# Twenty-one chunks of u turned by VectorE beside the mixer, not eighteen, at starts listed one by one

## The chip, the core and the metric

One core of a Trainium2 chip runs the kernel. The metric is the device time of one execution in microseconds (us). Three runs of the kernel before took 941.5, 942.26 and 942.73 us; their median is 942.26 us. The engines are named as in the profile: PE is TensorE, PEld its weight loads, DVE is VectorE, ACT is ScalarE, POOL is GpSimd, SP is SyncE, which here only issues transfers. ACT issues transfers too; "ACTq" and "SPq" mark these in the timelines.

## What is computed

One decoder layer on 256 tokens of width 1024, all in float32:

```python
h = rmsnorm(x, mix_norm_g[l])
proj = h @ w_in[l]
rq, rk, rv, rg, mq, mk, mv, ga, gb = jnp.split(proj, offsets, axis=-1)
...
y_a = (from_heads(ret) * jax.nn.silu(rg)) @ ret_w_branch[l]
...
y_b = from_heads(att) @ moba_w_branch[l]
merged = jax.nn.sigmoid(ga) * y_a + jax.nn.sigmoid(gb) * y_b
x = x + merged @ w_out[l]
h2 = rmsnorm(x, ffn_norm_g[l])
x = x + peer(h2, peer_w_q[l], peer_sub_keys[l], peer_u[l], peer_v[l])
```

`ret` is retention over two chunks of 128 tokens, `att` block-sparse attention. `peer` picks 16 of 16384 experts for each token and head, by keys:

```python
u = u_tab[ec]
a = jax.nn.gelu(jnp.einsum('td,thkd->thk', hc, u), approximate=False)
return jnp.einsum('thk,thkd->td', gc * a, v_tab[ec])
```

## The kernel before

The program is one stream of instructions for each engine, in the order of the code; what an engine has issued is never overtaken on that engine. The work has four stages.

**The mixer** (0 to about 240 us): everything up to `x + merged @ w_out`. Its weights are cut into 72 pieces, each 256 rows by 512 columns, held as 128 partitions x 1024. The first pieces are those of the attention's q, k and v, then come the retention's q, k and v (12 to 27), the merge gates and the swish gate (28 to 51), the branch weights (52 to 63) and w_out (64 to 71). Pieces 64 to 67 make the left half of the output columns, 68 to 71 the right half.

**The queries** (to about 300 us): 16 more pieces, w_q, handled in the same way.

**The u stage** (303.5 to about 650 us): all products of the tokens with the 128 chunks of u, 128 rows each. PE needs each chunk with its rows along the free axis. So for a plain chunk it first makes eight 128 x 128 transposes (L738, `transpose_u`), which ACT copies out of PSUM in two steps (L739), and then the products (L1290).

**The v stage** (about 650 to 930 us): the products with the 128 chunks of v (L1322 and L1323), and a tail.

Around the u and v stages POOL and DVE gather and treat rows for some of the tokens; the change touches none of that.

*The loop of the mixer* (L844) takes the pieces i in order, and its body sets the order of all queues:

```python
for i in range(n_mixer + 3):
    load_to(i + 1)
    ...
    cut(i + 3)
    products(i)
    early_turns(i)
    pump()
```

- `load_to` has SP load weights (L203) into a ring of six raw tiles, and goes four pieces ahead of the one that it is called for.
- `cut(i + 3)` splits a piece into an upper part, which ACT copies (`rhi`, L148), and a lower part, which DVE subtracts (`rlo`, L149); there are four of each, numbered on in the names that the trace prints. A piece's three products a tile (upper by upper, and both cross products) are L231 to L233 or L240 to L242.
- `products(i)` issues PE's work on piece i and, at the last piece of a unit, starts the unit's epilogue, a generator that goes on a step at each `pump()`. Two such generators matter here. `retention` makes scores, multiplies them by the decay on DVE in two halves (`st`, L431), multiplies by v on PE (L442) and normalises; ACT scales the result (`ret`, L462). `residual` adds the last products to the residual stream (`xt`, L563), weights it by the gain (`xg`, L567), both on DVE, and PE transposes it (L576) for the queries.
- `early_turns(i)` prepares chunks of u for the u stage. For such a chunk ACT issues four loads (L748, the quarters of the chunk, one for each 32 partitions and 128 KB each), DVE transposes the chunk in blocks of 32 x 32, in two half-turns at two successive i (`STREAM_TRANSPOSE`, L752, 128 x 512 each), and ACT issues the store of the turned chunk (L764) to a tensor in device memory. There are two pairs of buffers, `eraw` to `eT` and `h` to `hTf`, used by turns. A chunk's loads go out when the chunk before it starts its first half-turn. The loads of the next use of a buffer wait for the half-turns of the last one, and the half-turns into `eT` or `hTf` wait for its last store.

In the kernel before, chunk number m (0 to 17) makes its first half-turn at i = 14 + 3m, its second one piece later, its store two pieces later, and its loads go out three pieces earlier. Turned are the chunks 6, 13, 20 and so on to 125: one in seven (`STEP`). The u stage loads these from where they were stored (`turned[c // STEP]`) and leaves out L738 and L739 for them.

Of the kernel before, what the change touches and what calls it, by code (L numbers as in the profile page):

```python
# [50 lines left out]
HELD = [0, 1, 2, 8, 14, 21] + list(range(26, 62, 6)) + [61, 66]  # L51
HELD0 = 2
FOLD = 48
NPRE = 18
STEP = 7
PRE0 = 14
PERIOD = 3
TURN = ()
WARM = 8
GROW = 96  # L60
# [16 lines left out]
def layer_kernel(ctx, tc, x, mix_norm_g, w_in, ret_w_branch, moba_q_gain, moba_k_gain, moba_w_branch,  # L77
                 rel_bias, w_out, ffn_norm_g, peer_w_q, peer_sub_keys, peer_u, peer_v,
                 c_rope, c_decay, c_col, c_bucket, out, dbg=None):
    nc = tc.nc  # L80
# [23 lines left out]
    def raw_tile(n=1):  # L104

        i = raw_count[0] % RAWS
        raw_count[0] += n
        assert i + n <= RAWS
        return raw_ring[:, i] if n == 1 else raw_ring[:, i:i + n]
# [62 lines left out]

    turned = dr.tile([NPRE, P, D], F32, name="turned")
    ident = cp.tile([P, P], F32, name="ident")
# [37 lines left out]
    def products(i):  # L212
# [30 lines left out]
        if k0 + 2 == kc:  # L243
# [11 lines left out]
    early = ([ap.tile([P, D], F32, name="eraw"), h2],  # L255
             [ap.tile([P, D], F32, name="eT"), hTf.rearrange("p k t -> p (k t)")[:, :D]])
# [433 lines left out]
    def load_any(i):  # L690
# [9 lines left out]
        elif i < len(pieces) + NK:  # L700
# [3 lines left out]
            if early_chunk(c):  # L704
                u_raw[c] = raw_tile()
                nc.sync.dma_start(u_raw[c], turned[c // STEP])
            elif c in TURN:
# [33 lines left out]
    def early_chunk(c):  # L741
        return c % STEP == STEP - 1 and c // STEP < NPRE

    def load_quarters(queue, dst, c):

        src = peer_u[0, c * P:(c + 1) * P, :].rearrange("(b a) (g d) -> g a b d", a=32, g=4)
        for g in range(4):
            queue.dma_start(dst[32 * g:32 * g + 32].rearrange("a (b d) -> a b d", b=4), src[g])  # L748

    def turn(dst, src, k):  # L750

        V.transpose(dst.rearrange("p (k b a) -> p b k a", k=KC, b=4)[:, :, k],  # L752
                    src.rearrange("p (b k i) -> p b k i", b=4, k=KC)[:, :, k])

    def early_turns(i):

        m, step = divmod(i - PRE0, PERIOD)
        if step == 0 and -1 <= m < NPRE - 1:
            load_quarters(nc.scalar, early[0][(m + 1) % 2], STEP * (m + 1) + STEP - 1)
        if 0 <= m < NPRE:  # L760
            if step < 2:
                turn(early[1][m % 2], early[0][m % 2], slice(4 * step, 4 * step + 4))
            if step == PERIOD - 1:
                nc.scalar.dma_start(turned[m], early[1][m % 2])  # L764

    G.iota(jp, pattern=[[1, P]], base=0, channel_multiplier=-1)
# [559 lines left out]
    for c in range(NK):  # L1326
# [14 lines left out]
        if c == FOLD:  # L1341
            assert gs["sum"] >= NV - NJ
            for b in range(KC):
                s = slice(b % 4 * 32, b % 4 * 32 + 32)
# [111 lines left out]
```

## Time and profile before

| what | value |
|---|---|
| median of the three runs | 942.26 us |
| the profiled execution, its own time | 945.16 us |
| its span | 943.3 us |
| granted clock of PE | 1.0 |
| instructions | 19128 |
| moved | 322.56 MB, 342 GB/s over the span |
| transfers issued by ACT's queue (q10) | 21.29 MB, 7.5% of the 16 engines' span |

The page's slices give each engine's busy share in tenths over 40 equal stretches of the span, here 23.6 us each, and what the transfers moved:

```profile
PE   9999999999999999999999999999999999999997
...
DVE  6658557788678998999998999974978988899978
ACT  6544655544644435444687778776454636464443
...
DMA  9899779998799998999999999999999999999994
```

The mixer is the first ten digits. A timeline's row reads: start, duration, engine, line and operation, output and inputs; a count behind "x" is the number of records drawn together into one row. In square brackets stands how long the engine was idle before, and what came last of what it waited for.

### The profile page before, as it was taken

Reading aid. Unit: us, or ns where it says so; the run is one execution under the profiler, and the core shown is the slowest. Engines: PE = TensorE matmul, PEld = TensorE weight load, DVE = VectorE, ACT = ScalarE, POOL = GpSimd, SP = SyncE. Lnnn points to the kernel's source line nnn. Section 1 sums busy time; section 2 is a strip of 40 time slices with the busy share of each in tenths; the row PEclk is TensorE's granted clock in tenths of the full one; section 3 lists DMA queues with packets and bytes.
Section 4 is the critical chain, followed back from the end, with each engine's and each line's share of the span. In section 5 each row is a group of like instructions: output and inputs, shape, how many; then the busy total and the mean of one; then the engine's idle time right before and its main releaser. Section 6 shows DMA issues by size and latency. Waiting matters only on the chain.

```text
span 943.3 us, 19128 instructions
## 1 busy us (share of the span) xinstructions
PE 933.2 (99%) x7192; PEld 893.3 (95%) x7192; DVE 793.5 (84%) x1521; ACT 520.9 (55%) x953; POOL 399.6 (42%) x313
## 2 busy tenths in 40 slices
PE   9999999999999999999999999999999999999997
PEld 6887898998999999999999999999999999999996
DVE  6658557788678998999998999974978988899978
ACT  6544655544644435444687778776454636464443
POOL 3412010000202446534646677763546555575721
PEclk9999999999999999999999999999999999999999
DMA  9899779998799998999999999999999999999994
GB/s 320 232 235 283 241 206 291 303 300 264 244 363 379 403 402 274 403 406 359 377 398 391 377 363 382 377 386 364 362 357 402 409 377 367 406 402 392 409 337 134
DMA packets 111050, 322.56 MB, mean 342 GB/s; under 512 B 11660, under 2 KB 23861, under 8 KB 110830
## 3 DMA queue, kind: packets, MB, share of 16 engines
q1 hardware_dynamic: 64460, 184.38, 55.0%
q0 software_dynamic: 32752, 115.67, 32.5%
q10 hardware_dynamic: 13746, 21.29, 7.5%
q8 instruction: 57, 0.93, 0.4%
q14 instruction: 35, 0.29, 0.1%
HBM read 308.63 MB, written 14.19 MB: 342 GB/s over the span
## 4 chain that ended last, share of the span: by engine, by line
PE 85%; DMA 7%; DVE 3%; issue 2%; POOL 1%; ACT 1%; SPq 0%; DVEq 0%; ACTq 0%; POOLq 0%
PE acc L1290 24%; PE side L738 11%; PE acc L1322 7%; PE side L1322 7%; DMA raw_ring<-in_peer_v_dram 5%; PE acc L231 5%; PE acc L232 5%; PE acc L233 5%; PE acc L1323 3%; PE side L1323 3%; PE acc L240 3%; PE acc L241 3%; PE acc L242 3%; DMA bias<-skew 1%; PE acc L1218 1%
## 5 line engine op out<-in xcount | busy, mean ns | idle before, releaser
L1038 POOL DMA_INDIRECT rows<-in_peer_u_dram,eg x86 | 109.0, 1267 | 69.8 <-DVE rows L1049 32.6
L1038 POOL DMA_INDIRECT rows<-in_peer_v_dram,eg x54 | 99.8, 1849 | 74.2 <-DVE vacc L1124 47.9
L738 PE MATMUL side<-ident,raw_ring 128*128 128x128 f32 x768 | 103.0, 277 | 0.0
L738 PEld LDWEIGHTS side<-ident,raw_ring 128*128 128x128 f32 x768 | 93.0, 192 | 0.0
L1167 ACT ACTIVATE oh_buf<-oh_more,tS 128x128 bf16<-128x128 f16 x176 | 58.5, 417 | 0.5 <-issue 0.5
L1049 DVE SCALAR_TENSOR_TENSOR rows<-rows,h 128x1024 f32<-128x1024 f32 x43 | 53.0, 1244 | 2.9 <-DMA rows<-in_peer_u_dram,eg 2.9
L1124 DVE SCALAR_TENSOR_TENSOR vacc<-rows,av,vacc 128x1024 f32<-128x1024 f32 x43 | 55.0, 1279 | 0.1
L1262 ACT ACTIVATE cw<-W 128x352 fp32r<-128x352 f32 x58 | 28.7, 494 | 46.2 <-PE acc L1323 39.2
L1248 POOL TENSOR_TENSOR W<-W,gl 128x256 f32<-128x256 f32 (+19 forms) x31 | 25.5, 821 | 43.0 <-ACT gl L1247 35.1
L1263 DVE TENSOR_TENSOR cw<-W,cw 128x352 fp32r<-128x352 f32 x58 | 30.1, 519 | 15.8 <-ACT cw L1262 14.4
L581 POOL DMA_DIRECT2D x1d<-xt x1 | 0.7, 657 | 88.5 <-DVE xt L563 88.5
L1290 PE MATMUL acc<-hTd,raw_ring 128*128 128x128 f32 x288 | 35.1, 275 | 0.0
L1162 DVE TENSOR_TENSOR oh_more<-iota,tI 128x1024 f16<-128x1024 f16 x44 | 34.3, 779 | 0.0
L1163 DVE TENSOR_TENSOR oh_buf<-oh_more,tM 128x1024 f16<-128x1024 f16 x44 | 32.3, 734 | 2.2
L1290 PEld LDWEIGHTS acc<-hTd,raw_ring 128*128 128x128 f32 x288 | 33.6, 192 | 0.0
L155 POOL TENSOR_TENSOR gny<-va,minus_half 128x8 f32<-128x8 f32 x2 | 4.3, 2126 | 66.7 <-DVE va L455 66.7
L1217 PE MATMUL acc<-oh_buf 128*128 128x128 bf16 x176 | 24.4, 219 | 0.0
L1218 PE MATMUL acc<-oh_buf 128*128 128x128 bf16 x176 | 24.4, 219 | 0.0
L1231 ACT ACTIVATE W<-acc 128x512 f32<-128x512 f32 (+20 forms) x44 | 17.2, 390 | 11.9 <-PE acc L1218 7.1
L1250 ACT ACTIVATE W<-acc 128x256 f32<-128x256 f32 (+19 forms) x52 | 18.5, 356 | 4.4 <-PE acc L1290 4.4
L1233 DVE TENSOR_TENSOR W<-acc,W 128x264 f32<-128x264 f32 (+19 forms) x32 | 16.2, 507 | 4.8 <-ACT W L1231 4.4
L1217 PEld LDWEIGHTS <-oh_buf 128*128 128x128 f16 x176 | 19.8, 113 | 0.0
(2697 smaller groups left out, 3483.5 us busy)
## 6 DMA issues: line engine op xcount, KB each, us to landing
raw_ring<-in_peer_v_dram SPq DMA_DIRECT2D x128, 512.0 KB
raw_ring<-in_peer_u_dram SPq DMA_DIRECT2D x96, 512.0 KB
raw_ring<-in_w_in_dram SPq DMA_DIRECT2D x52, 512.0 KB
raw_ring<-turned SPq DMA_DIRECT2D x18, 512.0 KB
raw_ring<-in_peer_w_q_dram SPq DMA_DIRECT2D x16, 512.0 KB
W<-in_peer_u_dram SPq DMA_DIRECT2D x14, 512.0 KB
eraw<-in_peer_u_dram ACTq DMA_DIRECT2D x36, 128.0 KB
h<-in_peer_u_dram ACTq DMA_DIRECT2D x36, 128.0 KB
```

Source lines behind the costliest of these rows:

```text
L231: T.matmul(o[t], xh[:, s], wh, start=(k == 0), stop=False)
L232: T.matmul(o[t], xh[:, s], wl, start=False, stop=False)
L233: T.matmul(o[t], xl[:, s], wh, start=False, stop=(k == kc - 1))
L738: T.transpose(p[:, k * P:(k + 1) * P], r.rearrange("p (i k) -> p k i", k=KC)[:, 4 * q + k], ident)
L1038: G.indirect_dma_start(out=r, out_offset=None, in_=tab, in_offset=bass.IndirectOffsetOnAxis(ap=eg[:, j:j + 1], axis=0))
L1049: V.scalar_tensor_tensor(r, r, 1.0, h, op0=OP.mult, op1=OP.mult, accum_out=av[:, j:j + 1])
L1124: V.scalar_tensor_tensor(a, r, av[:, j:j + 1], a, op0=OP.mult, op1=OP.add)
L1167: A.activation(o1[:, j], hot[:, 0, :, j], AF.Copy, scale=tS[:, t, k + j:k + j + 1])
L1217: T.matmul(p[:, j * P:(j + 1) * P], hi, o1, start=True, stop=False)
L1290: T.matmul(pa[:, n:n + NA], uT[:, k * P:(k + 1) * P], hT[:, k], start=(c % 2 == 0 and k == 0), stop=(k == KC - 1), skip_group_check=True)
L1322: T.matmul(o[b][:, :2 * ND], vh[:, n], w, start=(c == 0), stop=False, skip_group_check=True)
L1323: T.matmul(o[b][:, :ND], vl[:, n], w[:, :ND], start=False, stop=(c == NK - 1), skip_group_check=True)
```

## The change

The number of chunks turned early goes from 18 to 21 (`NPRE`), and one chunk in six is such a chunk, not one in seven (`STEP`): 5, 11, 17 and so on to 125. The starts are no longer 14 + 3m but stand in a list. It begins with the same seven, 14 to 32, goes on with 34, 36, 38, 40 and 42, and then by threes from 45 to 69, where the starts before were 35, 38, 41 and so on to 65. The store goes out two pieces after the start as before or, where the next chunk starts two pieces later, with the second half-turn.

```diff
-NPRE = 18
-STEP = 7
-PRE0 = 14
-PERIOD = 3
+NPRE = 21
+STEP = 6
+STARTS = [14, 17, 20, 23, 26, 29, 32, 34, 36, 38, 40, 42, 45, 48, 51, 54, 57, 60, 63, 66, 69]
...
-        m, step = divmod(i - PRE0, PERIOD)
-        if step == 0 and -1 <= m < NPRE - 1:
-            load_quarters(nc.scalar, early[0][(m + 1) % 2], STEP * (m + 1) + STEP - 1)
-        if 0 <= m < NPRE:
-            if step < 2:
+        begun = [STARTS[0] - 3] + STARTS
+        if i in begun[:NPRE]:
+            m = begun.index(i)
+            load_quarters(nc.scalar, early[0][m % 2], STEP * m + STEP - 1)
+        for m in range(NPRE):
+            step = i - STARTS[m]
+            if step in (0, 1):
                 turn(early[1][m % 2], early[0][m % 2], slice(4 * step, 4 * step + 4))
-            if step == PERIOD - 1:
+            if i == min([STARTS[m] + 2] + [s - 1 for s in STARTS[m + 1:m + 2]]):
                 nc.scalar.dma_start(turned[m], early[1][m % 2])
```

A line is gone near the head of the file, so most line numbers of the changed kernel are lower by one (L148 is L147); from `early_turns` on they are higher by one.

**ACT, pieces 37 to 42.** Before, from the upper half of piece 37 (rhi__1226; 1268, 1308, 1340, 1359 and 1407 are pieces 38 to 42). A row "x4" on h or eraw is a set of quarter loads, "turned" a store, ah belongs to the attention:

```order
86 L148 ACTIVATE rhi__1226<-raw_ring 128x1024
87 L764 DMA turned<-eT 128x1024
88 L148 ACTIVATE ah<-side 128x4x128
89 L462 ACTIVATE ret<-side,nm,gny 128x128 x4
90 L148 ACTIVATE rhi__1268<-raw_ring 128x1024
91 L513 ACTIVATE sa<-acc 128x512 x2
92 L748 DMA eraw<-in_peer_u_dram 32x4x256 x4
93 L462 ACTIVATE ret<-side,nm,gny 128x128 x4
94 L148 ACTIVATE rhi__1308<-raw_ring 128x1024
95 L148 ACTIVATE rhi__1340<-raw_ring 128x1024
96 L764 DMA turned<-hTf 128x1024
97 L148 ACTIVATE rhi__1359<-raw_ring 128x1024
```

Now, from the set that stands ahead of ah (rhi__1273, 1310, 1346 and 1366 are pieces 38 to 41):

```order
88 L747 DMA eraw<-in_peer_u_dram 32x4x256 x4
89 L147 ACTIVATE ah<-side 128x4x128
90 L461 ACTIVATE ret<-side,nm,gny 128x128 x4
91 L147 ACTIVATE rhi__1273<-raw_ring 128x1024
92 L512 ACTIVATE sa<-acc 128x512 x2
93 L765 DMA turned<-hTf 128x1024
94 L461 ACTIVATE ret<-side,nm,gny 128x128 x4
95 L147 ACTIVATE rhi__1310<-raw_ring 128x1024
96 L747 DMA h_75<-in_peer_u_dram 32x4x256 x4
97 L147 ACTIVATE rhi__1346<-raw_ring 128x1024
98 L765 DMA turned<-eT 128x1024
99 L147 ACTIVATE rhi__1366<-raw_ring 128x1024
```

A store stands ahead of the second `ret` instead of a set, and a set now stands between pieces 39 and 40, where nothing stood.

**DVE, around the scores `st` of retention's second half.** Before (rlo__1309, 1341 and 1360 are the lower halves of pieces 39 to 41):

```order
100 L149 TENSOR_TENSOR rlo__1269<-raw_ring,rhi__1268 128x1024
101 L752 STREAM_TRANSPOSE hTf<-h_75 128x4x4x32
102 L149 TENSOR_TENSOR rlo__1309<-raw_ring,rhi__1308 128x1024
103 L752 STREAM_TRANSPOSE hTf<-h_75 128x4x4x32
104 L431 TENSOR_TENSOR st<-side,decay 128x512
105 L149 TENSOR_TENSOR rlo__1341<-raw_ring,rhi__1340 128x1024
106 L431 TENSOR_TENSOR st<-side,decay 128x512
107 L149 TENSOR_TENSOR rlo__1360<-raw_ring,rhi__1359 128x1024
```

Now:

```order
101 L148 TENSOR_TENSOR rlo__1274<-raw_ring,rhi__1273 128x1024
102 L751 STREAM_TRANSPOSE hTf<-h_75 128x4x4x32
103 L148 TENSOR_TENSOR rlo__1311<-raw_ring,rhi__1310 128x1024
104 L751 STREAM_TRANSPOSE eT<-eraw 128x4x4x32
105 L430 TENSOR_TENSOR st<-side,decay 128x512
106 L148 TENSOR_TENSOR rlo__1347<-raw_ring,rhi__1346 128x1024
107 L751 STREAM_TRANSPOSE eT<-eraw 128x4x4x32
108 L430 TENSOR_TENSOR st<-side,decay 128x512
```

A half-turn has come in between piece 40's lower half and the second `st`.

**ACT, around the first residual.** Before, from the last set (rhi__2087 is piece 66, 2125 to 2181 are pieces 67 to 70; `mh` is the merged branch, `sq` the square that follows xt):

```order
149 L748 DMA h_75<-in_peer_u_dram 32x4x256 x4
150 L148 ACTIVATE rhi__2087<-raw_ring 128x1024
151 L148 ACTIVATE mh_138<-sa 128x512 x2
152 L148 ACTIVATE rhi__2125<-raw_ring 128x1024
153 L764 DMA turned<-eT 128x1024
154 L148 ACTIVATE rhi__2145<-raw_ring 128x1024
155 L148 ACTIVATE rhi__2163<-raw_ring 128x1024
156 L148 ACTIVATE rhi__2181<-raw_ring 128x1024
157 L569 ACTIVATE sq_2201,ss_117<-xt 128x512
```

Now (rhi__2096 is piece 66, 2138 to 2198 are pieces 67 to 70):

```order
153 L147 ACTIVATE rhi__2096<-raw_ring 128x1024
154 L147 ACTIVATE mh_138<-sa 128x512 x2
155 L747 DMA h_75<-in_peer_u_dram 32x4x256 x4
156 L147 ACTIVATE rhi__2138<-raw_ring 128x1024
157 L147 ACTIVATE rhi__2158<-raw_ring 128x1024
158 L765 DMA turned<-eT 128x1024
159 L147 ACTIVATE rhi__2176<-raw_ring 128x1024
160 L747 DMA eraw<-in_peer_u_dram 32x4x256 x4
161 L147 ACTIVATE rhi__2198<-raw_ring 128x1024
162 L568 ACTIVATE sq_2218,ss_117<-xt 128x512
```

Two sets have come in: one behind `mh`, ahead of piece 67, and one ahead of piece 70.

**SP, the loads of weights in the denser stretch.** The order is the same; in brackets stands what each load waits for (DMAHW with a number is a counter of completed transfers). Before:

```order
51 L203 DMA raw_ring<-in_w_in_dram 128x2x512 [waits DMAHW1_49,DVE_49]
52 L203 DMA raw_ring<-in_w_in_dram 128x2x512 [waits DMAHW3_49,DMAHW2_49,DVE_49]
53 L203 DMA raw_ring<-in_w_in_dram 128x2x512 [waits DMAHW5_49,DVE_49]
54 L203 DMA raw_ring<-in_w_in_dram 128x2x512 [waits DMAHW1_49,DVE_49]
55 L203 DMA raw_ring<-in_w_in_dram 128x2x512 [waits DMAHW3_49,DVE_49]
56 L203 DMA raw_ring<-in_w_in_dram 128x2x512 [waits DMAHW5_49,DVE_49]
```

Now:

```order
51 L202 DMA raw_ring<-in_w_in_dram 128x2x512 [waits DMAHW3_49,DVE_49]
52 L202 DMA raw_ring<-in_w_in_dram 128x2x512 [waits DMAHW7_49,DMAHW2_49,DVE_49]
53 L202 DMA raw_ring<-in_w_in_dram 128x2x512 [waits DMAHW5_49,DMAHW2_49,DVE_49]
54 L202 DMA raw_ring<-in_w_in_dram 128x2x512 [waits DMAHW6_49,DMAHW1_49,DVE_49]
55 L202 DMA raw_ring<-in_w_in_dram 128x2x512 [waits DMAHW4_49,DMAHW1_49,DVE_49]
56 L202 DMA raw_ring<-in_w_in_dram 128x2x512 [waits DMAHW5_49,DMAHW0_49,DVE_49]
```

Nothing has moved, but rows 52 to 56 now wait for two such counters each, where before row 52 alone did.

## The prediction

> **What bounds the kernel.** I read the busy times first, then busy time by stage, then the timelines of TensorE (PE), VectorE (DVE) and ScalarE (ACT) side by side.
>
> ```profile
> PE 933.2 (99%) x7192; PEld 893.3 (95%) x7192; DVE 793.5 (84%) x1521; ACT 520.9 (55%) x953; POOL 399.6 (42%) x313
> ```
>
> ```profile
> core 0: us, PE busy (x) PEld busy (x) DVE busy (x) ACT busy (x) POOL busy (x), PEclk, DMA share, GB/s
> 140.00:160.00 20.00, 20.00 (x108) 16.83 (x107) 14.29 (x32) 11.11 (x19) 1.64 (x1) 1.00 1.00 268
> 220.00:240.00 20.00, 20.00 (x92) 16.15 (x91) 16.13 (x21) 10.97 (x15) 0.00 (x0) 1.00 0.75 244
> 303.50:650.00 346.50, 346.50 (x3265) 346.50 (x3265) 318.24 (x841) 217.00 (x536) 198.65 (x178) 1.00 0.98 376
> 650.00:930.00 280.00, 278.10 (x2028) 276.88 (x2027) 250.30 (x249) 144.51 (x174) 154.12 (x84) 1.00 0.99 378
> ```
>
> PE works 933.2 of 943.3 us. It is never free in the two mixer windows shown (140 to 160, 220 to 240) or in the u stage (303.5 to 650), always at a granted clock of 1.00. So any PE work removed comes off the time, and any wait put in front of PE goes on it, one for one. A busy PE does not say how near the others are to holding it up; the timelines below do.
>
> **What goes.** Three more chunks of u reach the u stage turned, so PE leaves out 3 x 8 transposes (L738), and ACT 3 x 2 copies. In the timeline of PE, the transposes of two chunks and the products of two:
>
> ```profile
> 457.67 1.05 PE L738 MATMUL side<-ident,raw_ring 128*128 128x128 f32 x8
> 458.55 1.95 PE L1290 MATMUL acc<-hTf,rhi__4949 128*128 128x128 f32 x16
> 460.34 1.05 PE L738 MATMUL side<-ident,raw_ring 128*128 128x128 f32 x8
> 461.23 1.95 PE L1290 MATMUL acc<-hTd,raw_ring 128*128 128x128 f32 x16
> ```
>
> ```profile
> L738 PE MATMUL side<-ident,raw_ring 128*128 128x128 f32 x768 | 103.0, 277 | 0.0
> ```
>
> Eight transposes push the next work back from 457.67 to 458.55 and from 460.34 to 461.23, by 0.88 and 0.89 us; a chunk's sixteen records of products take 1.79 (458.55 to 460.34). Three chunks: 3 x 0.89 = **2.67 us** gone. The 277 ns that the group has for one transpose is the time through the pipeline: 768 of them were busy for 103.0 us only. The Trainium skill, "TensorE: Matmul & The Clock Gate", section Part 4, PE-mode transpose, gives some 275 ns for one in a kernel's context; by it 24 would be 6.6 us and the sum below about 939.0. The rows here disagree: the records overlap, and eight take 0.88. I use the rows.
>
> The u stage has PE at 346.50 of 346.50, so nothing there is known to hide the gain. What is late next are the chunk loads (DMA share 0.98 at 376 GB/s) and, after the stage, those of v (0.99). I take nothing for it: in the v stage PE idles 280.00 - 278.10 = 1.9 us in all. If DMA were the bound there, the whole 2.67 would come back as waits; that is a rival.
>
> **What comes.** All of it stands beside the mixer, the first 240 us: three more sets of four quarter loads and three more stores in ACT's queue, six more half-turns on DVE, and 3 x (0.5 + 0.5) MB of transfers. From piece 34 to 42 the sets come every two pieces, not every three, and afterwards the rest of the row stands at other pieces than before. What one costs:
>
> ```profile
> L752 DVE STREAM_TRANSPOSE hTf<-h x18: 698/704/707, 71.2 to 227.8; 128x512 f32<-128x512 f32 x18
> ```
>
> ```profile
> 118.48 3.15 ACTq L748 DMA_DIRECT2D h<-in_peer_u_dram  x4
> ...
> 151.22 1.91 ACTq L748 DMA_DIRECT2D eraw<-in_peer_u_dram  x4
> ...
> 212.13 2.03 ACTq L748 DMA_DIRECT2D h<-in_peer_u_dram  x4
> ```
>
> Six half-turns are 6 x 0.704 = 4.2 us of DVE, in windows where it has 4 to 6 of 20 us free; in amount that is hidden. A set of loads holds ACT's queue for 1.9 to 3.15 us, because ACT itself issues the four; over the sets I read the mean is 2.3. What stands behind it in ACT's order waits so long. Mostly that is the upper half of a piece of weights (L148), and DVE's lower half (L149) follows it. From the end of the lower half to PE's first product on it, most pieces have 4 to 7 us, which hides one set: piece 39's ends at 139.55 (below), and PE takes it at 145.38. I look for the places where it is not so.
>
> ```profile
> 145.38 0.50 PE L231 MATMUL acc<-rhi__1308,hh 128*128 128x512 f32 x1
> ```
>
> **Place one: retention, second half, at 142.41 us.** PE needs the second score tile st from DVE. (rhi__1308, 1340, 1359 and 1407 are the upper halves of pieces 39 to 42.)
>
> ```profile
> 137.22 1.07 ACT L148 ACTIVATE rhi__1308<-raw_ring 128x1024 fp32r<-128x1024 f32 x1
> 138.16 1.07 ACT L148 ACTIVATE rhi__1340<-raw_ring 128x1024 fp32r<-128x1024 f32 x1
> 140.20 0.35 ACTq L764 DMA_DIRECT2D turned<-hTf  x1
> 140.67 1.07 ACT L148 ACTIVATE rhi__1359<-raw_ring 128x1024 fp32r<-128x1024 f32 x1 [1.44 <-DMA raw_ring<-in_w_in_dram]
> 140.70 2.87 ACTq L748 DMA_DIRECT2D h<-in_peer_u_dram  x4
> 143.69 1.06 ACT L148 ACTIVATE rhi__1407<-raw_ring 128x1024 fp32r<-128x1024 f32 x1 [1.95 <-DMA raw_ring<-in_w_in_dram]
> ```
>
> ```profile
> 138.32 1.23 DVE L149 TENSOR_TENSOR rlo__1309<-raw_ring,rhi__1308 128x1024 fp32r<-128x1024 f32 x1 [2.33 <-ACT rhi__1308 L148]
> 139.46 0.70 DVE L752 STREAM_TRANSPOSE hTf<-h 128x512 f32<-128x512 f32 x1
> 140.09 0.65 DVE L431 TENSOR_TENSOR st<-side,decay 128x512 f32<-128x512 f32 x1
> 140.66 1.21 DVE L149 TENSOR_TENSOR rlo__1341<-raw_ring,rhi__1340 128x1024 fp32r<-128x1024 f32 x1
> 141.79 0.68 DVE L431 TENSOR_TENSOR st<-side,decay 128x512 f32<-128x512 f32 x1
> ```
>
> ```profile
> 142.41 1.95 PE L442 MATMUL side<-rv,st 128*128 128x128 f32 x16
> ```
>
> The rows show both ways in which ACT is held. A store waits for its half-turn (139.46 to 140.16) and goes at 140.20, and the ACTIVATE behind it starts only at 140.67. A set issued from 140.70 to 143.57 lets the next ACTIVATE go at 143.69; the weights named as its releaser had been asked for long before. PE's first eight records at 142.41 use the first st, so the second is wanted near 143.3, and it was ready at 142.47: 0.8 us of cover.
>
> Now a store (of the chunk before) stands ahead of the second retention scaling and of piece 39, which I put 0.9 us later (138.1); the set h stands between pieces 39 and 40, so piece 40's upper half goes at 138.1 + 2.3 = 140.4 and ends at 141.5; its lower half ends at 142.7; then comes the added half-turn, to 143.4, and st, to 144.05. Late by 144.05 - 143.3, with the handing over about **1.0 us**. Bounds: a set of 1.9 us and a store that costs nothing give 0, a set of 3.15 us 1.7.
>
> **Place two: the first residual, at 231.50 us.** PE transposes xg, which stands behind four other steps in DVE's queue. (rhi__2125 and 2181 are pieces 67 and 70.)
>
> ```profile
> 221.38 0.63 ACT L148 ACTIVATE mh<-sa 128x512 fp32r<-128x512 f32 x1 [2.08 <-DVE sa L550]
> 221.92 1.04 ACT L148 ACTIVATE rhi__2125<-raw_ring 128x1024 fp32r<-128x1024 f32 x1
> ...
> 226.22 1.06 ACT L148 ACTIVATE rhi__2181<-raw_ring 128x1024 fp32r<-128x1024 f32 x1 [0.35 <-ACT rhi__2163 L148]
> ```
>
> ```profile
> 228.46 1.19 DVE L149 TENSOR_TENSOR rlo__2182<-raw_ring,rhi__2181 128x1024 fp32r<-128x1024 f32 x1
> 229.56 1.28 DVE L563 TENSOR_TENSOR xt<-xt,acc 128x512 f32<-128x512 f32 x2
> 230.76 1.28 DVE L567 TENSOR_TENSOR xg<-xt,grow 128x512 f32<-128x512 f32 x2
> ```
>
> ```profile
> 231.50 1.26 PE L576 MATMUL side<-ident,xg 128*128 128x128 f32 x8
> ```
>
> DVE works without a gap here, and the first xg ends at 230.76 + 0.64 = 231.40, 0.1 us before PE takes it: there is no slack at all. Before, no set of loads was issued between 214.2 (the last, at 212.13) and this place. Now two stand there: one right behind mh, ahead of piece 67's upper half, one ahead of piece 70's. With sets of D1 and D2, pieces 67 to 69 go on ACT from 221.9 + D1 for 3 x 1.0 us, and 0.1 for the store between them; piece 70's starts after D2 and takes 1.1, its lower half 1.2, then xt 1.2 and the first xg 0.64: 229.2 + D1 + D2 in all. Late by D1 + D2 - 2.3 against 231.5, with 2.3 for each **2.3 us**. Bounds: both 1.9 give 1.5; both 3.15 give 4.0. It is nothing only if ACT runs ahead of this order, for instance if mh comes earlier; it waits for PE's products and DVE, so I see no reason for that.
>
> **Elsewhere.** Pieces 45 to 48 are ready 3.5 to 4.4 us early, the least of the dense part's end. The denser sets take about 2 us of it: 0, with an upper bound of 1. SP's loads of weights keep their order, but rows 52 to 56 of its order now wait for a second completion, which can be that of a set or a store. They are asked for 14 to 16 us ahead of their use, as far as I followed them, so I take 0; it is part of the same bound of 1. Later steps that PE waits for (the rotated and gated tiles) have no set in front that they did not have before, or more cover: 0.
>
> **The sum.** -2.67 + 1.0 + 2.3 = +0.6 us. Against the profiled execution's 945.16 us that is 945.8; on the median of the runs, 942.26, about 2.9 us lower as runs without the profiler are, **942.9 us**. A measurement of this kernel tells about 0.2%, 1.9 us, from no change: under 940.4 is faster, over 944.1 slower.
>
> **Rivals.**
> *The covers hold.* If both places cost under 0.8 us together, the gain of 2.67 stays: 939.6, up to 940.4. For it: all PE waits of the mixer were small before, and ACT is busy for only 11 of 20 us. Against it: the zero slack at 231.50, and the queue times above are not counted as ACT's busy time. That transposes are worth more than 0.11 us each, so that the time falls to about 939.0, has against it the rows at 457.67; I give it 0.01 within this case's 0.23.
> *Long sets in ACT's queue: slower.* The place is again the first residual, the price the two sets' issue time. From D1 + D2 of 5.9 us on (two of 2.95; 3.15 was seen once in the rows above), place two costs 3.6 and place one 1.3 or more; with 0 to 1.0 at pieces 45 to 48 the sum is +2.2 to +3.2: 944.5 to 945.5. For it: the same chunk halves are read by the loads while weights and stores are in flight, at a DMA share of 1.00 in the dense part. Against it: two long sets in a row are rare, and the window at 220 to 240 has a DMA share of 0.75. Chance 0.16.
> *The gain is given back.* The v stage is bound by its transfers (share 0.99, 378 GB/s), PE arrives 2.67 us earlier and waits as much more: 942.26 + 3.3 = 945.6. Against it: 1.9 us of idle PE in 280. Chance 0.08.
>
> **How the numbers follow.** The forecast (the places cost 0.8 to 4.5 us together, so 940.4 to 944.1) has 0.53, the covers 0.23, long sets 0.16, gain given back 0.08. Faster 0.23, same 0.53, slower 0.24. The range is from 939.4 (whole gain, and the spread of the runs) to 945.2, which leaves out most of the gain given back and the ends of the other two.
>
> **What would show it.** In the profile after: chunk starts 1.79 us apart at 21 chunks, not 18, and the u stage 2.7 us shorter; an idle stretch on PE ahead of the second half of L442 near 143 us and one ahead of L576 near 231, with DVE's xg as what ended it and a set of loads ahead of piece 70's upper half on ACT. If L576 starts right behind the products, place two is wrong; if the u stage is not shorter, the removed work was not the bound; if the v stage is longer by as much, the gain was given back.

## The result, and the profile after

| | before | after |
|---|---|---|
| median of seven runs each, us | 942.73 (941.5 to 945.25) | 948.91 (945.53 to 952.05) |
| ratio, with its 95% interval | | 1.0059 (1.0041 to 1.0078) |
| the profiled execution, its own time | 945.16 | 949.06 |
| its span | 943.3 | 947.3 |

The ratio is not the quotient of the two medians but an estimate of its own from the runs; here and below the two differ by up to 0.16%, 1.5 us. By the interval of the ratio the change makes the kernel slower by 3.9 to 7.4 us. The forecast was 942.9 in a range of 939.4 to 945.2: about 6 us too low, and the range did not reach the result.

The busy times of the changed kernel, and its windows (start:end, span, busy time of PE, PEld, DVE, ACT and POOL, granted clock, DMA share, GB/s):

```profile
PE 933.0 (98%) x7168; PEld 892.2 (94%) x7168; DVE 798.8 (84%) x1527; ACT 515.0 (54%) x947; POOL 395.4 (42%) x313
```

```profile
140.00:160.00 20.00, 19.30 (x104) 16.12 (x103) 13.80 (x32) 7.95 (x12) 1.65 (x1) 1.00 1.00 285
160.00:180.00 20.00, 19.21 (x118) 16.91 (x117) 16.92 (x22) 11.96 (x18) 0.00 (x0) 1.00 0.96 296
230.00:234.00 4.00, 3.74 (x17) 2.73 (x15) 2.46 (x3) 1.21 (x2) 0.00 (x0) 1.00 0.93 314
234.00:238.00 4.00, 1.54 (x7) 1.54 (x8) 4.00 (x7) 2.28 (x5) 0.00 (x0) 0.73 1.08 226
238.00:242.00 4.00, 4.00 (x18) 3.32 (x17) 3.83 (x5) 2.31 (x4) 0.00 (x0) 0.84 1.06 345
303.50:650.00 346.50, 345.63 (x3249) 345.06 (x3248) 321.95 (x860) 212.21 (x533) 201.60 (x181) 1.00 0.99 380
```

PE has 24 instructions fewer, the transposes of three chunks (7192 to 7168). It now has holes at 140 to 180 and a large one at 234 to 238, where the granted clock falls to 0.73; in the window after it is 0.84. The u stage, without a hole before, has one of 0.9 us. What ended the holes stands in the view of PE's waits (engine and line waited at, releaser, total, times, longest):

```profile
PE side L575 <- DVE xg L566: 2.7, 1, 2.7
...
PE acc L231 <- DVE rlo__1551 L148: 0.8, 1, 0.8
PE acc L1218 <- DVE W L1234: 0.8, 1, 0.8
PE side L441 <- DVE st L430: 0.7, 1, 0.7
```

Of these four none was there before. To see what each stretch lost, I take the starts of five of PE's steps from both timelines; a stretch is the difference of two starts:

| stretch on PE, from step to step | before | after | difference |
|---|---|---|---|
| retention's second half (L442, 142.41) to its state products (L447) | 1.88 | 2.81 | +0.93 |
| from there to the first residual's transposes (L576) | 87.21 | 91.23 | +4.02 |
| to the second residual's transposes | 12.26 | 13.41 | +1.15 |
| on to 255.75 (261.87 after), the first transposes of the query stage's keys | 11.99 | 12.00 | 0 |
| to the first product of the v stage (649.82, then 654.42) | 394.07 | 392.55 | -1.52 |
| v stage and tail, to the end of the span | 293.48 | 292.87 | -0.62 |

The rows sum to +3.96, the difference of the spans (947.3 - 943.3 = 4.0). I do not count the v stage's difference as part of the change: from its first to its last product the stage took 284.5 to 288.7 us in the profiles of all kernels here, with 288.7 before and 288.1 after, and no product of it was changed.

The place at the first residual, in the three timelines of the changed kernel. ACT:

```profile
223.77 0.63 ACT L147 ACTIVATE mh<-sa 128x512 fp32r<-128x512 f32 x1 [2.08 <-DVE sa L549]
223.77 1.77 ACTq L747 DMA_DIRECT2D h<-in_peer_u_dram  x4
225.67 1.06 ACT L147 ACTIVATE rhi__2138<-raw_ring 128x1024 fp32r<-128x1024 f32 x1 [1.27 <-DMA h<-in_peer_u_dram]
...
229.12 3.05 ACTq L747 DMA_DIRECT2D eraw<-in_peer_u_dram  x4
232.29 1.06 ACT L147 ACTIVATE rhi__2198<-raw_ring 128x1024 fp32r<-128x1024 f32 x1 [2.14 <-DMA raw_ring<-in_peer_w_q_dram]
```

DVE, and PE:

```profile
231.33 0.70 DVE L751 STREAM_TRANSPOSE hTf<-h 128x512 f32<-128x512 f32 x1
233.38 1.23 DVE L148 TENSOR_TENSOR rlo__2199<-raw_ring,rhi__2198 128x1024 fp32r<-128x1024 f32 x1 [1.35 <-ACT rhi__2198 L147]
234.53 1.28 DVE L562 TENSOR_TENSOR xt<-xt,acc 128x512 f32<-128x512 f32 x2
235.72 1.29 DVE L566 TENSOR_TENSOR xg<-xt,grow 128x512 f32<-128x512 f32 x2
```

```profile
236.46 1.97 PE L575 MATMUL side<-ident,xg 128*128 128x128 f32 x8 [2.73 <-DVE xg L566]
238.08 0.78 PE L230 MATMUL acc<-rhi__2176,mh 128*128 128x512 f32 x1
238.66 0.63 PE L231 MATMUL acc<-rlo__2177,mh 128*128 128x512 f32 x1
239.08 0.49 PE L232 MATMUL acc<-rhi__2176,ml 128*128 128x512 f32 x1
239.41 0.40 PE L230 MATMUL acc<-rhi__2176,mh 128*128 128x512 f32 x1
```

Read in order: the set at 223.77 holds piece 67 until 225.67, the set at 229.12 holds piece 70 until 232.29. DVE stands idle for 1.02 us ahead of piece 67's lower half (at 226.76, not shown) and for 1.35 us ahead of piece 70's, and xt and xg follow behind it. PE waits 2.73 us. Behind the wait its steps are slow: the eight transposes take 1.97 us where they took 1.26, and the first product 0.78, not 0.39. That is the lower clock of the windows at 234 and 238.

### The profile page after: what moved, and what is told of

It reads as the page before. It is cut to its first block, busy times and chain, and to the rows that moved or that the text cites. A ratio compares the mean times of both kernels' runs of the same rounds, so it can differ in the third digit from the quotient of the medians.

```text
span 947.3 us, 19094 instructions
## 1 busy us (share of the span) xinstructions
PE 933.0 (98%) x7168; PEld 892.2 (94%) x7168; DVE 798.8 (84%) x1527; ACT 515.0 (54%) x947; POOL 395.4 (42%) x313
## 4 chain that ended last, share of the span: by engine, by line
PE 81%; DVE 8%; DMA 6%; ACT 2%; issue 2%; ACTq 1%; POOL 0%; DVEq 0%; SPq 0%; POOLq 0%
PE acc L1291 21%; PE side L737 9%; PE acc L1323 8%; PE side L1323 8%; PE acc L230 4%; PE acc L231 4%; PE acc L232 4%; PE acc L1324 3%; PE side L1324 3%; DMA raw_ring<-in_peer_v_dram 3%; PE acc L239 2%; PE acc L240 2%; PE acc L241 2%; PE side L1321 2%; PE acc L1321 2%
## 5 line engine op out<-in xcount | busy, mean ns | idle before, releaser
L737 PE MATMUL side<-ident,raw_ring 128*128 128x128 f32 x744 | 99.9, 277 | 0.0
L737 PEld LDWEIGHTS side<-ident,raw_ring 128*128 128x128 f32 x744 | 90.2, 192 | 0.0
L1050 DVE SCALAR_TENSOR_TENSOR rows<-rows,h 128x1024 f32<-128x1024 f32 x43 | 54.6, 1284 | 0.0
L1291 PE MATMUL acc<-hTd,raw_ring 128*128 128x128 f32 x336 | 41.0, 275 | 0.0
L1291 PEld LDWEIGHTS acc<-hTd,raw_ring 128*128 128x128 f32 x336 | 39.2, 192 | 0.0
L1163 DVE TENSOR_TENSOR oh_more<-iota,tI 128x1024 f16<-128x1024 f16 x44 | 31.3, 711 | 0.0
L1218 PEld LDWEIGHTS <-oh_buf 128*128 128x128 f16 x176 | 19.8, 113 | 1.0 <-DVE W L1234 0.9
L1219 PEld LDWEIGHTS <-oh_buf 128*128 128x128 f16 x176 | 19.8, 114 | 0.0
L751 DVE STREAM_TRANSPOSE eT<-eraw 128x512 f32<-128x512 f32 x22 | 15.5, 705 | 3.9 <-DMA eraw<-in_peer_u_dram 2.2
```

What stands on the lines that cost most here:

```text
L737: T.transpose(p[:, k * P:(k + 1) * P], r.rearrange("p (i k) -> p k i", k=KC)[:, 4 * q + k], ident)
L1050: V.scalar_tensor_tensor(r, r, 1.0, h, op0=OP.mult, op1=OP.mult, accum_out=av[:, j:j + 1])
L1218: T.matmul(p[:, j * P:(j + 1) * P], hi, o1, start=True, stop=False)
L1219: T.matmul(p[:, j * P:(j + 1) * P], lo, o1, start=False, stop=True)
L1291: T.matmul(pa[:, n:n + NA], uT[:, k * P:(k + 1) * P], hT[:, k], start=(c % 2 == 0 and k == 0), stop=(k == KC - 1), skip_group_check=True)
```

## The experiments

The ratios below are against the kernel before on the same chip, with 95% intervals; medians of the kernel before were 941.4 to 942.6 us there. "PE waits" are from each run's profiled execution, a single one, which can be among the slowest of its kernel. Theory 1 is that of the prediction: the sets and stores in ACT's order delay pieces, and PE waits for them at places. Its rival is that each further chunk costs by its bytes and half-turns wherever it stands.

### The parts alone

The denser stretch alone, with 18 chunks:

```diff
-NPRE = 21
-STEP = 6
+NPRE = 18
+STEP = 7
-STARTS = [14, 17, 20, 23, 26, 29, 32, 34, 36, 38, 40, 42, 45, 48, 51, 54, 57, 60, 63, 66, 69]
+STARTS = [14, 17, 20, 23, 26, 29, 32, 34, 36, 38, 40, 42, 45, 48, 51, 54, 57, 60]
```

> The first 18 starts of the changed list (14 to 32 by threes, 34 to 42 by twos, 45 to 60 by threes), 18 turned chunks, one in seven: the denser stretch alone, with as many sets, half-turns, stores and bytes as before and the u stage as before. Theory 1 (the sets and stores in ACT's queue delay pieces that DVE and PE then wait for, place by place): waits on PE of about 0.9 us at the second half of retention (143 us) and about 1 us at piece 47 (168 us), none at the first residual, granted clock 1.0 throughout; about 1.5 to 2 us over the kernel before, 944.2 to 944.8. Theory 2 (the cost comes with the additional chunks: their bytes, half-turns and transfers): the kernel before, 942.7 within 0.7.

Measured 944.2 us, 1.0039 (1.0022 to 1.0056). PE waits 0.7 us for st at 143 and 1.1 us for piece 47 at 168; the clock is 1.00 and the first residual has no wait. The kernel is slower with no more chunks than before, as theory 1 says. Some of the twelve runs took 947 to 950 us, which the one profile does not explain.

The late starts alone, again with 18 chunks and one in seven:

```diff
+STARTS = [14, 17, 20, 23, 26, 29, 32, 35, 38, 41, 44, 47, 50, 57, 60, 63, 66, 69]
```

> 18 turned chunks, one in seven, by threes from 14 to 50 as before, then 57, 60, 63, 66, 69 as in the change: the late starts alone, with the bytes of before. Theory 1: no wait at 143 and 168 us; the sets issued at pieces 63 and 66 delay pieces 67 to 70 on ACT, so PE waits about 2.7 us for xg at the first residual, and the granted clock is below 1 for some us behind it, another 1.2 us: 946 to 947.5. Theory 2: 942.7 within 0.7. If the late wait is there but without the lower clock, 945.4.

Measured 946.77 us, 1.0041 (1.0026 to 1.0055). No wait at 143 and 168, and 3.0 us at the first residual. The second set took 3.56 us here, and the clock fell to 0.55 and 0.59 in the two windows of 2 us behind the wait. That is theory 1 again.

The saving alone:

```diff
-                nc.sync.dma_start(u_raw[c], turned[c // STEP])
+                nc.sync.dma_start(u_raw[c], turned[min(c // STEP, len(STARTS) - 1)])
```

with the starts 14 + 3m of before in the list, and the loops of `early_turns` over these 18 alone. It leaves out turning the last three chunks, so its output is not the layer's; its work on PE in the u stage is that of the change.

> The mixer of the kernel before (18 chunks turned, starts 14 + 3m), but the u stage takes 21 chunks as turned, one in six; the last three (chunks 113, 119, 125) are read from the place of the eighteenth. Turning them is left out. Theory 1: the u stage is 2.67 us shorter and the time falls by 2 to 2.7 us: 940.0 to 940.8. Rival (the v stage is bound by its transfers and gives the gain back): u stage 2.67 us shorter, v stage as much longer, 942.7 within 0.5.

Measured 939.58 us, 0.9974 (0.9963 to 0.9986): 1.3 to 3.5 us faster. The v stage does not give it back. But the u stage is 1.1 us shorter in the profile, not 2.67, since a new wait stands in it:

```profile
PE acc L1218 <- DVE W L1234: 1.0, 2, 0.8
```

DVE's own rows there, in the changed kernel, show no idle time on DVE:

```profile
588.00 1.21 DVE L1050 SCALAR_TENSOR_TENSOR rows__6430<-rows__6430,h 128x1024 f32<-128x1024 f32 x1
...
589.65 1.16 DVE L1193 TENSOR_SCALAR gl<-tS 128x48 int32<-128x48 int32 x1
...
592.16 0.69 DVE L1164 TENSOR_TENSOR oh_buf<-oh_more,tM 128x1024 f16<-128x1024 f16 x1
592.77 0.57 DVE L1234 TENSOR_TENSOR W<-acc,W 128x408 f32<-128x408 f32 x1
```

and PE's:

```profile
590.65 2.00 PE L1291 MATMUL acc<-hTf,rhi__6605 128*128 128x128 f32 x16
593.40 0.25 PE L1218 MATMUL acc<-oh_buf 128*128 128x128 bf16 x1 [0.75 <-DVE W L1234]
```

In this stretch DVE works through two products with gathered rows (L1050) and the preparation of the next gates without a pause, and W is the last of it. PE comes 0.75 us too early. Where DVE sets the pace, a chunk's transposes saved on PE are only waited for. The runs without this wait bear that out: in the one with 24 further products below, which has none, the stretch from the second residual to the v stage is 2.55 us shorter than before, nearly the 2.67 of the forecast, and in the changed kernel 1.51.

### The idle time and the clock

24 further products on PE ahead of the transposes, which the transposes then overwrite:

```diff
                 p = side()
+                for k in range(24 if j == 0 and t == 0 else 0):
+                    T.matmul(p[:, :P], ident, ident, start=True, stop=True)
```

> The changed kernel with 24 further products of 128 x 128 x 128 (identity by identity) on PE ahead of the first transposes of the first residual, written to the tile that the transposes then overwrite. They take about 2.6 us and lie in PE's wait there of 2.7 us. Theory 1 with the clock as its second part (the granted clock falls because PE stands idle): the wait stays, the clock stays at 1.0 behind it, and the time is about 1.2 us under the changed kernel, 947.5. Rival (the lower clock has nothing to do with the idle time, or the filler isn't hidden): the clock falls as before and the time is 948.9 or up to 2.6 us more.

Measured 947.7 us, 1.0059 (1.0039 to 1.0078). The 24 products were 48 records and took 5.4 us, twice what I had reckoned, so they outlast the wait. The clock stays at 1.00 throughout. This is not decisive for the time.

The changed kernel once more, and 11 such products:

> The changed kernel once more, so that the three below have it on their chip. By the parts measured (late starts +4.8, denser stretch +2.2, u stage -2.4) 4.6 us over the kernel before; its first measurement was 6.2 over. The granted clock is under 1.0 behind PE's wait of 2.7 to 3 us at the first residual.

> As the run with 24 further products, but 11 of them: 24 took 5.4 us (two records each), so 11 should take 2.5 us and lie wholly in PE's wait of 2.7 us. Theory 1 (idle PE lowers the clock): the transposes start no later than in the changed kernel, the clock stays at 1.0, and the time is 1 to 1.2 us under the changed kernel on the same chip. Rival: the clock falls all the same and the time is that of the changed kernel.

Measured 948.28 us, 1.0053 (1.0034 to 1.0073), for the changed kernel; a wait of 2.9 us for xg, and 14.89 us from the first to the second residual, 2.6 more than before. With 11 products 948.51 us, 1.0061 (1.0038 to 1.0084): the wait is filled, the clock is 1.00 there, the stretch is 12.27 us, as before the change, and yet the time is the same. So filling PE's wait keeps the clock up, but I could not see it in the time. Both profiled executions are among the slowest of their kernel (952.83 and 952.72 us) and have further waits and further falls of the clock. In the changed kernel's second measurement it fell early on, too, to 0.53 from 12 to 14 us, behind a wait of 1.3 us for POOL. With 11 products it fell near 484 us, to 0.50, behind a wait of 1.8 us for DVE.

The same question in a kernel with that wait only, the late starts with 18 chunks, with and without 11 products:

> The run with the late starts alone (18 chunks, one in seven, starts by threes to 50, then 57 to 69), with 11 products of identity by identity on PE in the wait of 3.0 us at the first residual, 2.5 us of work. If idle PE lowers the clock and that is paid: clock 1.0, and 1.2 to 2.6 us under the same kernel without them, beside it here: 944 to 945.5 where the kernel before takes 942. Rival (not paid, or made up for later by the transfers in the v stage): as without them.

> The run with the late starts alone once more, beside the one before on its chip: 3.9 to 4.8 us over the kernel before as in its first measurement, a wait of 3.0 us at the first residual and a clock under 1.0 behind it.

Measured 946.57 us, 1.0044 (1.0029 to 1.006), with them and 946.64 us, 1.004 (1.0026 to 1.0054), without, where the wait was 2.3 us this time, not 3.0. These are the windows with the wait unfilled:

```profile
230.00:234.00 4.00, 2.10 (x10) 1.40 (x8) 2.85 (x5) 1.89 (x4) 0.00 (x0) 1.00 1.02 308
234.00:238.00 4.00, 3.61 (x13) 3.23 (x14) 3.91 (x6) 3.46 (x6) 0.00 (x0) 0.57 1.07 315
```

and filled:

```profile
230.00:234.00 4.00, 4.00 (x30) 3.69 (x29) 2.51 (x4) 1.71 (x4) 0.00 (x0) 1.00 0.94 294
234.00:238.00 4.00, 3.80 (x23) 2.98 (x22) 4.00 (x6) 3.46 (x7) 0.00 (x0) 1.00 1.07 303
```

The clock falls to 0.57 in the one and stays in the other, and the stretch to the second residual is 13.72 against 12.27 us. The medians differ by 0.07 us. Either the 1.45 us is made up for later, or the spread of the runs (3 to 4 us) hides it: that stays open. The mean clock of each run points the same way: it is at most 0.998 in all ten runs of the changed kernel's second measurement and in only two of the ten with 11 products, and yet their medians are 948.28 and 948.51 us.

### Where the sets are issued

All sets of loads from POOL's queue:

```diff
-            load_quarters(nc.scalar, early[0][m % 2], STEP * m + STEP - 1)
+            load_quarters(nc.gpsimd, early[0][m % 2], STEP * m + STEP - 1)
```

> The changed kernel with the four quarter loads of each set issued by POOL's queue, which has nothing to do from 100 to 240 us, not ACT's. Theory 1 (the sets' issue time in ACT's order is what delays pieces 67 to 70): no wait of PE at the first residual or under 0.5 us, clock 1.0; the waits at 143 and 168 us shrink to under 0.5 us each; 940 to 941.5 where the kernel before takes 942. Theory 2 (the transfers themselves, or DVE's further half-turns, are the cost): the waits stay within 0.5 us of the changed kernel's. A third way: POOL's own work between 45 and 100 us (rotary products) comes later behind the sets' waits, and PE waits there, anew.

Measured 941.75 us, 0.998 (0.9962 to 0.9998), with every half-turn, store and byte of the change. PE's waits in the mixer:

```profile
PE side L416 <- ACT rv L467: 0.8, 1, 0.8
PE side L597 <- DVE hn L587: 0.4, 1, 0.4
...
PE side L441 <- DVE st L430: 0.3, 1, 0.3
```

The waits at the first residual and at piece 47 are gone, that for st is 0.3 us. From 100 us on a set takes POOL 2.18 to 2.24 us. This run speaks for theory 1 at the first residual and at piece 47: with the same bytes and the same work on DVE the change loses nothing there once ACT does not issue the sets. One thing did change with the queue: the 84 loads went as 4032 packets, where ACT's queue sent 12096. That packets and not the place of issue are the cause is not excluded by this run alone; the run with the earlier dense stretch below, with 21 sets on ACT and no wait at these two places, speaks against it. The time is level with the kernel before or slightly under it.

Only the last set from POOL's queue, and then the last two (`m > NPRE - 3`):

```diff
+            load_quarters(nc.gpsimd if m == NPRE - 1 else nc.scalar, early[0][m % 2], STEP * m + STEP - 1)
```

> The changed kernel with one set alone, the last (issued at piece 66, ahead of piece 70's upper half), on POOL's queue, the other twenty on ACT's as in the change. Theory 1 (the two sets ahead of pieces 67 and 70 add up in one chain of ACT and DVE, late by D1 + D2 - 2.3): with D1 of about 1.8 alone nothing is late, no wait at the first residual over 0.3 us, clock 1.0 behind it, so the stretch from the group norm's products to the first residual is about 2.7 us shorter and the next one 1.2 to 2.6: 3.9 to 5 us under the changed kernel, 943.5 to 944.5 where that took 948.3 and the kernel before 942. Rival (it is the half-turns on DVE in that place, or the bytes in flight): the wait stays over 2 us and the time at 947 to 948.

Measured 945.14 us, 1.0024 (1.0009 to 1.0039), with a wait of 1.3 us at the first residual, where I expected none, and no lower clock:

```profile
PE side L575 <- DVE xg L566: 1.3, 1, 1.3
```

```profile
227.93 1.23 DVE L148 TENSOR_TENSOR rlo__2139<-raw_ring,rhi__2138 128x1024 fp32r<-128x1024 f32 x1 [1.18 <-ACT rhi__2138 L147]
```

ACT's chain alone would have had room for a set of 1.94 us. But DVE had none: from piece 67's lower half on it works through eight steps to xg, and they took 8.1 us before the change (223.28 to 231.40) with one pause of 0.5. So a delay of piece 67 (here DVE stood idle for 1.18 us ahead of its lower half, rlo__2139) goes straight through, and the second set adds its own on top.

> The changed kernel with its last two sets (issued at pieces 63 and 66) on POOL's queue, the other nineteen on ACT's. Neither delays pieces 67 to 70, so no wait at the first residual over 0.3 us and clock 1.0 behind it; the waits at 143 and 168 us and the u stage stay. If the lower clock is paid: 4 to 5.4 us less than the changed kernel's 5.0 to 6.2 over the kernel before, so 0.2 to 1.5 over it. If only the wait of 2.8 us is paid: 2.2 to 3.4 over it.

Measured 944.7 us, 1.0023 (1.001 to 1.0035); no wait at the first residual. Against the two ratios of the changed kernel (1.0053 and 1.0059) the late place costs 0.30 to 0.36%, 2.8 to 3.4 us. That is near the wait of 2.7 to 2.9 us, but the intervals leave some 2 us to either side, so it does not tell whether the clock is paid on top. By the losses reckoned so far (0.93 + 1.2 - 1.52) the run should have been 0.6 us over the kernel before; it is 0.9 to 3.3 over. Its profile shows two more: from the second residual to the u stage's first products it takes 60.63 us, not 59.78, with a wait of 0.6 us ahead of the last transposes before them for which no releaser is shown, and from the start of PE's last product of the v stage to the end 5.50 us, not 4.75. Whether other executions have these is not known.

The sets from piece 32 on from POOL, the first seven from ACT; and the same with the chunks 4, 10 to 124 (`STEP - 2` for `STEP - 1`):

```diff
+            load_quarters(nc.gpsimd if m > 6 else nc.scalar, early[0][m % 2], STEP * m + STEP - 1)
```

> The changed kernel with the sets of chunks 7 to 20 (those issued from piece 32 on) on POOL's queue, the first seven on ACT's as before. Theory 1: as with all sets on POOL, no wait at the first residual and at piece 47 and 0.5 us at 143 us, and without that run's 0.8 us of PE waiting for ACT ahead of retention (its first sets were late behind POOL's rotary work): 0.8 us under that run, 1.3 per mille under to 3.7 under the kernel before: 939 to 941.2. Rival (that wait has another cause): as that run, 941.7.

> As the run before, with the turned chunks 4, 10, 16 and so on to 124 in the place of 5, 11, 17 to 125. In all runs with one chunk in six so far PE waited 0.8 us near 590 us for DVE's scaling of the gates, right behind the products of a turned chunk, where DVE worked without a gap: the saving of that chunk was lost. If the place of the turned chunk decides it, the wait moves or shrinks and the u stage is up to 0.9 us shorter: 0 to 0.9 us under the run before. Rival (DVE's whole work sets the pace around there): the same wait at another chunk, no difference.

Measured 946.85 us, 1.0046 (1.0027 to 1.0065), and 947.06 us, 1.0049 (1.0033 to 1.0065). Both missed. PE did not wait for ACT ahead of retention any more, and neither at the first residual nor at piece 47. But from the start of PE's last product of the v stage to the end of the span it was 9.8 us in both, against 4.9 in the run with all sets on POOL and 4.8 before. In the trace POOL's closing drain, its last long instruction, takes 10.03 to 10.04 us there, against 4.99 in the kernel before. The total time therefore hides what else these two runs would tell. The profiles still answer the question of the second: with the chunks 4 to 124 the wait for W near 590 us is gone, where the first has 0.7 us, and the stretch from the second residual to the v stage is 404.56 us, not 405.83, though a new wait of 1.0 us for ACT stands in it before 560 us.

All sets from POOL, with chunks 4, 10 to 124:

> All 21 sets on POOL's queue, and the turned chunks 4, 10, 16 and so on to 124. In the two runs before, with 56 transfers more on POOL than in the changed kernel, POOL's closing drain took 10.0 us where the changed kernel's takes 5.0, and this alone ended those runs late; with 84 more it took 3.9. If the drain goes by the number of POOL's transfers it is 3.9 here, and with the mixer of the run with all sets on POOL and a u stage 0.5 to 1.3 us shorter the time is 940.4 to 941.7 where the kernel before takes 942. Rival (the drain has to do with the place of the turned chunks or varies from build to build): a drain of 10, 946 to 947.

Measured 940.65 us, 0.9995 (0.998 to 1.001). The drain is 3.84 us, with as many transfers on POOL as in the first such run. The u stage's wait for W is down to 0.2 us, and the stretch from the keys' transposes to the v stage is 391.83 us against 393.33 in that run. In the total, this run is level with the kernel before; the two arrangements can't be told apart.

### An earlier dense stretch

```diff
+STARTS = [14, 17, 20, 22, 24, 26, 28, 30, 32, 34, 36, 38, 41, 44, 47, 50, 53, 56, 59, 62, 65]
```

> 21 chunks, one in six, with the denser stretch earlier: starts 14, 17, 20, then every two pieces from 22 to 38, then by threes from 41 to 65, as the last nine before. A piece lasts 3 to 5 us there, not 2.7, and weights are ready 4 to 12 us ahead. Theory 1: no wait at the first residual and at piece 47, at most 1 us around 143 us, u stage 2.67 us shorter: 939.5 to 941 where the kernel before takes 942. Theory 2 (cost by the number of chunks): about the changed kernel, 946 to 948.

Measured 944.35 us, 1.0012 (0.9994 to 1.0031). No wait at piece 47 or the first residual, so those two go by place, not by the number of chunks. But three waits stand around retention, 0.8 (L416), 1.1 (L428) and 0.7 us (L441), and with the u stage's 0.8 they cancel the saving. The time lies between the two expectations: I had reckoned the slack of the weights there, and not that retention's own chain has little.

## Why the prediction was wrong

Term by term, the forecast against the changed kernel's stretches:

| term, us | forecast | in the trace |
|---|---|---|
| transposes left out | -2.67 | -1.52 |
| place one | +1.0 | +0.93 |
| pieces 45 to 48 | 0 | +0.95 |
| place two | +2.3 | +2.73, and 0.34 more on the way to it |
| behind the wait, at the lower clock | none | +1.15 |
| sum | +0.6 | +4.6 |

**The step that failed** is the price of the sets in ACT's order, with what hangs on it. The forecast took each set as the 2.3 us of the kernel before and looked at each place alone. Behind piece 32 the ten sets of the kernel before took 1.8 to 3.0 us, 2.4 on average; the thirteen of the changed kernel took 1.8 to 5.0, 3.3 on average. So 0 for pieces 45 to 48 was wrong, and nothing stood in the sum for the stretch behind a wait on PE. The gain that DVE takes back in the u stage is the other term that was mis-sized.

**The removed work: right, over-sized.** The u stage was to be 2.67 us shorter. It is 1.5 us, and the view of the waits shows 0.8 us of PE waiting for DVE near 590. My sentence that the u stage hides none of the gain, since PE was at 346.50 of 346.50, was wrong at that place: a full PE did not mean that the engine behind it had room. That the v stage gives the whole gain back was a rival; the run with the saving alone, 1.3 to 3.5 us under the kernel before, refutes it.

**Place one: the number right, the path only in part, so partly by luck.** The forecast had the second st end at 144.05 and 1.0 us lost. DVE ended it at 143.37 + 0.65 = 144.02, and the stretch lost 0.93:

```profile
139.28 1.23 DVE L148 TENSOR_TENSOR rlo__1311<-raw_ring,rhi__1310 128x1024 fp32r<-128x1024 f32 x1 [2.92 <-ACT rhi__1310 L147]
140.42 0.70 DVE L751 STREAM_TRANSPOSE eT<-eraw 128x512 f32<-128x512 f32 x1
141.05 0.65 DVE L430 TENSOR_TENSOR st<-side,decay 128x512 f32<-128x512 f32 x1
141.62 1.21 DVE L148 TENSOR_TENSOR rlo__1347<-raw_ring,rhi__1346 128x1024 fp32r<-128x1024 f32 x1
142.75 0.70 DVE L751 STREAM_TRANSPOSE eT<-eraw 128x512 f32<-128x512 f32 x1
143.37 0.65 DVE L430 TENSOR_TENSOR st<-side,decay 128x512 f32<-128x512 f32 x1
```

The store made piece 39 late, as forecast, and the added half-turn came in. But the set between pieces 39 and 40, which the forecast had as the bound, did not set the time: ACT was through with piece 40's upper half at 140.90, and DVE, at work without a pause since 139.28, reached its lower half (rlo__1347) only at 141.62. With all sets on POOL these six steps take as long, 139.48 to 144.23 us, and PE's stretch still loses 0.56 us.

**Elsewhere: wrong.** I took 0 for pieces 45 to 48, with an upper bound of 1. PE lost 0.95 us at piece 47 in the changed kernel and about 1.2 in the dense stretch alone. What failed is "the denser sets take about 2 us of it". Piece 47's cover had been 3.5 us, and all of it went:

```profile
150.49 4.33 ACTq L747 DMA_DIRECT2D h<-in_peer_u_dram  x4
154.92 1.06 ACT L147 ACTIVATE rhi__1474<-raw_ring 128x1024 fp32r<-128x1024 f32 x1 [3.45 <-PE acc L232]
157.90 0.35 ACTq L765 DMA_DIRECT2D turned<-eT  x1
158.30 0.46 ACT L461 ACTIVATE ret<-side,nm,gny 128x128 f32<-128x128 f32 x1 [2.31 <-DVE nm L457]
```

A set takes 4.33 us, longer than any that I had quoted; why sets last longer in the changed kernel is open. The delayed piece delays the half-turn behind it on DVE; the store waits for that on ACT; and the retention's scaling and piece 45 wait for the store. ACT and DVE hand the lateness on to each other. Places reckoned one at a time do not show that.

**Place two: the mechanism right, the size wrong.** Forecast 2.3 us, "D1 + D2 - 2.3"; the wait is 2.7 to 2.9. With D1 alone it is 1.3 us, where the formula gives none: it followed ACT and took DVE's eight steps as free to run close up behind. So its 2.5 us for the sets measured, 1.77 and 3.05, come near the 2.73 partly by chance. Both sets were inside the bounds, which gave up to 4.0.

**Missing: the clock.** I had no term for what follows a wait on PE. In the traces the stretch behind the wait at the first residual is 1.15 to 2.6 us longer. The Trainium skill, "TensorE: Matmul & The Clock Gate", in the section on why this matters for your kernels, warns of gaps of over some 3 us between bursts of products. Here the clock fell after shorter waits, too: at the first residual after 2.3, 2.7, 2.9 and 3.0 us but not after 1.3, elsewhere once after 1.3 and once after 1.8, but not after 1.5 (at 12 us, in the run with the earlier dense stretch). The length of the last wait alone does not decide it.

**The rival that came nearest** is "long sets in ACT's queue", with 0.16. It had the right mechanism at the right place, but it asked for 5.9 us of sets there, where 1.77 + 3.05 = 4.8 were enough, and its 944.5 to 945.5 us were too low as well.

**The sum.** By the stretches the change costs 0.93 + 4.02 + 1.15 - 1.52 = 4.6 us; the runs say 3.9 to 7.4, and 5.0 (3.2 to 6.9) in the second measurement. So the losses shown are enough to make the kernel slower, and in the late place the run with the last two sets on POOL puts 2.8 to 3.4 us. Up to about 1.5 us in the runs with the denser stretch has no row that more than one profile shows, and whether the lower clock is paid is open. The 2.9 us that the forecast put down to the profiler are no fixed amount: the profiled execution took 939.47 us where its kernel's median is 940.65, and 945.31 where it is 941.75. As only the difference of +0.6 went into the forecast, that did no harm.

## What to carry to other kernels

Transfers that an engine issues are work in its order: four issues of 128 KB each held ACT's queue for 1.8 to 5.1 us without counting as busy time, and what stands behind them is late. Move them to a queue with nothing behind it before adding more, and look at the end of the program afterwards: 14 of the 21 sets on POOL's queue made it 5 us longer, all 21 did not. When slack is counted, follow the chain through every engine that passes it on, with the longest issue seen, and ask of a saving on a full engine who is next, place by place.

## What was not expected of the hardware

- POOL's closing drain took 4.99 us in the kernel before and in the changed one, and 4.99 to 5.80 in the others with as many transfers issued by POOL (261); 5.31 with 265, 5.72 with 269, but 10.03 to 10.04 with 317 and 3.84 to 3.86 with 345. Why is open.
- A set of four issues took 1.8 to 5.1 us on ACT's queue, longer in kernels with the late dense stretch than without it; on POOL's, 2.17 to 2.27 from 100 us on.
- The clock fell after PE waits of 2.3, 2.7, 2.9 and 3.0 us at the first residual, in all four traces that have such a wait there, and some 2.5 us of products of no use kept it up. Two more falls came after waits of 1.3 and 1.8 us, while other waits of 1.3 and 1.5 us had none. The trace has the clock at 0.50 for 3.4 us in each fall (235.9 to 239.3 us in the changed kernel), and for 6.8 us at the first residual in its second measurement.
